# A gating unit's values moved ahead of the attention, and a gelu written with the hyperbolic tangent

## The chip, the cores and the metric

The kernel runs on one core of one Trainium2 chip. The metric is the device time of one execution in microseconds (us). The kernel before took 2144.43, 2147.16 and 2149.66 us in three runs; the median is 2147.16.

## The reference, cut to what matters

The program computes two stacks of two layers each on 256 tokens of width 1024. The change touches the mixer of the first stack (`first_block`), which runs once per layer. The mixer normalises its input, projects it with `w_in`, and splits the result for three units: a chunked spatial gating (a), a recurrence (b) and a sparse attention (c). Their outputs stand side by side and are projected back with `w_out`.

```python
def chunked_spatial_gating(z_a, ln_g, ln_b, w_s, b_s):
    u, v = split_cols(jax.nn.gelu(z_a), A_SIZES)
    u = u.reshape(Bn, nc, CHUNK, A_HEADS, HEAD_DIM)
    v = layer_norm(v.reshape(Bn, nc, CHUNK, A_HEADS, HEAD_DIM), ln_g, ln_b, LN_EPS)
    w = jnp.where(causal[None], w_s, 0.0)
    mixed = jnp.einsum('hts,bnshd->bnthd', w, v) + b_s.T[None, None, :, :, None]
    return (u * mixed).reshape(Bn, S, A_WIDTH)

for i in range(DEPTH):                        # DEPTH = 2
    z = rms_norm(h, g_mix[i]) @ w_in[i]
    z_a, z_b, z_c = split_cols(z, (A_COLS, B_COLS, C_COLS))
    y_a = chunked_spatial_gating(z_a, ...)    # 4 heads of 64
    y_b = rwkv7_time_mix(z_b, ...)            # 4 heads of 64, a state carried along the tokens
    y_c = nsa_attention(z_c, ...)             # 8 heads: compressed, selected and windowed keys
    h = h + jnp.concatenate([y_a, y_b, y_c], axis=-1) @ w_out[i]
    ...                                       # feed-forward (dense, then 8 experts) and one more gate
```

`jax.nn.gelu` is here the form 0.5 x (1 + tanh(sqrt(2/pi) (x + 0.044715 x^3))). The gating works per chunk of 128 tokens: it takes the values v, mixes them over the tokens of the chunk with a causal matrix, adds a bias, and multiplies by u.

## The kernel before, in words

All weights come from HBM as 32-bit numbers into raw tiles (`raw`), by loads that SyncE (SP) issues in a fixed order. Each raw tile is split into a high and a low part (`hl`): ScalarE (ACT) writes the high part, VectorE (DVE) the rest (`parts`, L392 and L393). A projection is then three matmuls for each product, so one of the 256-column projections `proj_fm` or `proj_tm` is 48 matmuls (`pj<-hl,xn` or `pj<-xn,hl`, `xn` being the normalised input).

`mix1` is the mixer. It projects the recurrence's input, runs the recurrence (`rwkv`, tiles in the bank `rw`), and projects for the other two units: `kv` (4), the queries `qT` (8 and 9), the values `vt` with the attention's gates, then, after the compression of keys and values (`nsa_cmp`), the gating's values `av` (5), the keys `ks` (7). Inside the attention (`nsa`), after the first of two halves of its heads, the function `between` projects the gating's other operand `uT` (6) and runs `gating`. The attention computes scores (`ns<-ks,qT`) with a mask (`ns<-cb,idb`), the maximum and exponential (L1139, L1142), transposes the weights and multiplies by the values (`py<-pT,vt`). `rows_out` and `route` multiply the result `y` with `w_out` (`pj<-y,hl`, `rw<-y,hl`); their first matmuls need only the recurrence's part of `y`.

`nsa_cmp` multiplies the keys and values by `cw1` in 32 steps (`ns<-cw,xp`), applies gelu (`hid`), transposes, multiplies by `cw2` (`kcT`, `vc`), scores against `qT` (`ns<-kcT,qT`), and takes an exponential (`pc`), whose transposes become `pcT`. The recurrence's output `yv` is normalised per head by `head_rs` (from the squares `gsq` to the reciprocal root `hrs`). `y` lies in a pool with one buffer (`act`) in which `xn` lies too, so it is written once the last reader of `xn` is done.

In `gating`, `gmws` (the mixing matrix) and `gmln` (the norm's gain and bias) are loaded, GpSimd masks `gmws`, ACT applies gelu to `uT` and `av`, DVE takes statistics per token and head (`gst`, `gmv`), ACT the root (`grs`), and DVE the four steps to `gvn` (L824 to L827). PE multiplies `ns<-gmws,gvn`, DVE adds the bias and multiplies by `uT` (`gm`), and `gm` becomes two of the eight parts of `y`.

The order of instructions on each engine is set when the program is built. A scheduler starts from the order of the code and lets an instruction that is ready pass one that is not, so that projections are strewn as fillers between the steps of the recurrence and of the attention. Each engine then works through its list in order; waits are for semaphores of other engines and of loads. ACT holds one table of functions at a time; a function of another table is preceded by ACT_TABLE_LOAD. Exponential and gelu need different tables here, and so does the root.

Of the kernel before, what the change touches and what calls it, by code (L numbers as in the profile page):

```python
# [28 lines left out]
AF = mybir.ActivationFunctionType  # L29
OP = mybir.AluOpType  # L30
AX = mybir.AxisListType

T = 256
# [249 lines left out]
class K:  # L283
# [511 lines left out]

    def gating(self, L, uT, v, y):

        nc, a = self.nc, self.a
        ws = self.t([128, 4, 128], "n2", "gmws")
        nc.sync.dma_start(ws, a["gmws"][L])  # L800
        lnb = self.t([128, 2, 256], "n2", "gmln")
        src = a["gmln"][L:L + 1]
        nc.sync.dma_start(lnb, bass.AP(tensor=src.tensor, offset=src.offset, ap=[[0, 128], [1, 512]]))
        bs = self.t([128, 2, 128], "n1", "gmbs")
        for h in range(4):
            src = a["gmbs"][L, h:h + 1]
            nc.sync.dma_start(bs[64 * (h % 2):64 * (h % 2) + 64, h // 2],
                              bass.AP(tensor=src.tensor, offset=src.offset, ap=[[0, 64], [1, 128]]))
        nc.gpsimd.tensor_tensor(ws, ws, self.cc("up_i").unsqueeze(1).to_broadcast([128, 4, 128]), op=OP.mult)
        nc.scalar.activation(uT, uT, AF.Gelu_apprx_tanh)  # L810
        nc.scalar.activation(v, v, AF.Gelu_apprx_tanh)
        st = self.t([128, 8, 6], "s", "gst")
        mv = self.t([128, 8, 2], "s", "gmv")
        v8 = v.rearrange("p j (h d) -> p (j h) d", h=4)
# [4 lines left out]
        rs = self.t([128, 8], "s", "grs")  # L819
        nc.scalar.activation(rs, mv[:, :, 1], AF.Sqrt, bias=self.cc("vec")[:, 4:5])  # L820
        nc.vector.reciprocal(rs, rs)
        vn = self.t([128, 2, 256], "n2", "gvn")
        vn8 = vn.rearrange("p j (h d) -> p (j h) d", h=4)
        nc.vector.tensor_tensor(vn8, v8, mv[:, :, 0:1].to_broadcast([128, 8, 64]), op=OP.subtract)  # L824
        nc.vector.tensor_tensor(vn8, vn8, rs.unsqueeze(2).to_broadcast([128, 8, 64]), op=OP.mult)
        nc.vector.tensor_tensor(vn, vn, lnb[:, 0:1].to_broadcast([128, 2, 256]), op=OP.mult)
        nc.vector.tensor_tensor(vn, vn, lnb[:, 1:2].to_broadcast([128, 2, 256]), op=OP.add)  # L827
        ps = self.bank("ns")
# [7 lines left out]
        mf = m.rearrange("p i j t -> p i (j t)")  # L836
        nc.vector.tensor_tensor(mf, mf, uT, op=OP.mult)
        self.dump(f"ya{L}", mf)
# [250 lines left out]
    def head_rs(self, s, scale, bias, floor=None):  # L1089


        nc, V = self.nc, self.nc.vector
# [4 lines left out]
        r = self.t([128, 8], "s", "hrs")  # L1097
        src = ps[:, :8]
        if floor is not None:
            V.tensor_scalar(r, src, floor, None, op0=OP.max)  # L1100
            src = r
        nc.scalar.activation(r, src, AF.Sqrt, scale=scale, bias=bias)
        V.reciprocal(r, r)
        p = self.bank("rw")
# [249 lines left out]
    def mix1(self, L, nxt):  # L1354
        a = self.a
        tp = self.tc.tile_pool
        with self.phase(f"m{L}", M1BANKS, "left", nm="ns", **M1ACC):
            with tp(name=f"wr{L}", bufs=1, reuse_waits="tile", side="right") as self.wr, \
                    tp(name=f"wp{L}", bufs=1, reuse_waits="tile") as self.wp:
                if L == 0:  # L1360
                    x = self.setup()
                else:
                    x = self.norm(self.pp(f"g_mix{L}", 0, 8))
# [19 lines left out]
                self.cycle = ("pj", "py")  # L1383
                self.proj_fm(a["w_in"][L, 4], x, kv)
                self.proj_fm(a["w_in"][L, 8], x, qT[:, 0:2])
                self.proj_fm(a["w_in"][L, 9], x, qT[:, 2:4])
                gps = self.t([128, 2, 24], "s4", "gps")
                self.proj_wide(a["w_vt"][L], x, vt, 24, gps)
                self.cycle = ("pj",)
                gt, vc, pcT = self.nsa_cmp(L, qT, kv, gps)  # L1390
                self.apply_rope(qT, qT, 0, "rp1")
                self.proj_tm(a["w_in"][L, 5], x, av)
                self.proj_fm(a["w_in"][L, 7], x, ks)
# [631 lines left out]
```

## Time and profile before

| | |
|---|---|
| median of three runs | 2147.16 us |
| the profiled execution's own time | 2147.74 us |
| its span | 2146.0 us |
| busy: PE, DVE, ACT | 96%, 77%, 60% of the span |
| mixer of layer 0 / layer 1 | about 0 to 206 / 420 to 640 us of the span |
| layer 1: first scores, then the product of the gating | 559.12, then 585.82 us |

The profile shows one execution, taken from the hardware. Rows of a timeline give start, duration, engine, line in the code, operation, the tiles (out<-in) and a count; in square brackets stands how long the engine waited before it and for whom. A matmul of 32-bit numbers that the code issues once can stand as two records. The granted clock of PE is 1.00 at its higher level (2.4 GHz) and 0.5 at its lower (1.2 GHz); a window with both lies between.

### The profile page before, as it was taken

How to read it: one execution, taken by the hardware profiler on the slowest of the kernel's cores; microseconds unless marked ns; L12 is line 12 of the kernel's file. 1: busy time of each engine (PE TensorE's matmuls, PEld its weight loads, DVE VectorE, ACT ScalarE, POOL GpSimd, SP SyncE). 2: the span in 40 equal slices, each digit the busy share in tenths (PEclk: the TensorE clock that was granted, in tenths of full speed). 3: DMA queues.
4: the chain of work that ended last, by engine and by line, in shares of the span. 5: the costliest groups of instructions: out<-in, count | busy, mean ns of one | idle time of the engine just before them, and what ended most of it. 6: DMA issues, size and time to landing. Idle time of an engine off the chain costs nothing.

```text
span 2146.0 us, 35556 instructions
## 1 busy us (share of the span) xinstructions
PE 2062.1 (96%) x14040; PEld 1828.6 (85%) x14040; DVE 1649.9 (77%) x2416; ACT 1292.8 (60%) x1914; POOL 28.6 (1%) x32
## 2 busy tenths in 40 slices
PE   7999999999898999999999999998999999999998
PEld 7877999988687888887887888787988999989998
DVE  7657888775747998989899888987858887756554
ACT  6347544552567777777877787776546444545443
POOL 0100000020000000000000000000000000000000
PEclk9999999999989999999999999998998999998999
DMA  6225999341426999899898989884347995435551
GB/s 244 83 70 187 322 341 331 136 151 52 177 84 221 367 347 340 337 367 338 335 355 340 369 322 358 345 325 148 122 179 265 349 337 185 130 138 167 187 182 55
DMA packets 106654, 519.84 MB, mean 242 GB/s; under 512 B 12400, under 2 KB 14448, under 8 KB 72432
## 3 DMA queue, kind: packets, MB, share of 16 engines
q1 hardware_dynamic: 106480, 517.50, 66.1%
q8 instruction: 112, 1.84, 0.3%
q14 instruction: 62, 0.51, 0.1%
HBM read 516.40 MB, written 1.05 MB: 241 GB/s over the span
## 4 chain that ended last, share of the span: by engine, by line
PE 62%; DVE 4%; ACT 2%; issue 1%; DVEq 0%; ACTq 0%
PE ps L346 37%; PE acc L346 17%; PE pj L346 3%; PE ac L346 2%; PE ns L346 2%; DVE hl L393 2%; PE ps L1624 1%; DVE ch L1697 1%; ACT hl L392 1%; PE py L346 0%; DVE xT L1603 0%; DVE xT L746 0%; ACT sq L565 0%; DVE xn L521 0%; PE ns L1155 0%
## 5 line engine op out<-in xcount | busy, mean ns | idle before, releaser
L393 DVE TENSOR_TENSOR hl<-raw,hl 128x1024 fp32r<-128x1024 f32 (+1 forms) x862 | 1028.9, 1224 | 222.6 <-ACT hl L392 217.9
L392 ACT CAST hl<-raw 128x1024 fp32r<-128x1024 f32 (+1 forms) x862 | 878.0, 1051 | 386.0 <-PE ps L346 193.3
L346 PE MATMUL ps<-hl,xe 128*128 128x512 f32 x2112 | 519.0, 400 | 6.3 <-ACTq L1639 4.2
L346 PEld LDWEIGHTS ps<-hl,xe 128*128 128x128 f32 x2112 | 390.6, 188 | 97.4 <-DVE hl L393 4.4
L346 PE MATMUL ps<-xn,hl 128*128 128x256 f32 x3552 | 433.2, 283 | 5.0 <-ACT xn L604 2.9
L346 PEld LDWEIGHTS ps<-xn,hl 128*128 128x128 f32 x3552 | 428.9, 191 | 6.3 <-ACT xn L604 3.5
L346 PE MATMUL acc<-hl,h 128*128 128x512 f32 x1056 | 262.2, 396 | 0.5 <-ACT h L1627 0.5
L346 PEld LDWEIGHTS acc<-hl,h 128*128 128x128 f32 x1056 | 198.7, 188 | 48.8 <-ACT h L1627 0.7
L346 PE MATMUL acc<-h,hl 128*128 128x256 f32 x1584 | 196.3, 283 | 0.0
L346 PEld LDWEIGHTS acc<-h,hl 128*128 128x128 f32 x1584 | 192.6, 192 | 0.2
L1668 DVE SCALAR_TENSOR_TENSOR junk<-raw,cact 128x1024 bf16<-128x1024 f32 x96 | 117.1, 1220 | 1.6 <-ACT cact L1662 0.7
L346 PE MATMUL pj<-xn,hl 128*128 128x256 f32 x720 | 102.9, 292 | 1.7 <-ACT xn L604 1.1
L346 PEld LDWEIGHTS pj<-xn,hl 128*128 128x128 f32 x720 | 92.6, 194 | 6.3 <-issue 3.9
L1620 ACT ACTIVATE s<-ps 128x256 f32<-128x256 f32 x88 | 33.9, 385 | 85.3 <-PE ps L346 85.2
L1627 ACT CAST h<-ps 128x256 fp32r<-128x256 f32 x88 | 32.7, 372 | 50.8 <-PE ps L1624 50.7
L1697 DVE SCALAR_TENSOR_TENSOR ch<-hp,par,ch 128x256 f32<-128x256 f32 x120 | 51.1, 477 | 0.0
L346 PE MATMUL ns<-xn,hl 128*128 128x256 f32 x288 | 40.0, 301 | 10.6 <-ACT hl L392 8.6
L346 PEld LDWEIGHTS ns<-xn,hl 128*128 128x128 f32 x288 | 38.5, 208 | 11.3 <-ACT hl L392 8.6
L346 PE MATMUL ac<-xn,hl 128*128 128x256 f32 x336 | 46.9, 290 | 0.3 <-ACT xn L604 0.3
L346 PE MATMUL pj<-y,hl 128*128 128x256 f32 x288 | 45.0, 293 | 0.9 <-ACT y L406 0.9
L346 PE MATMUL pj<-hl,xn 128*128 128x256 f32 (+2 forms) x288 | 44.4, 297 | 0.0
L346 PEld LDWEIGHTS ac<-xn,hl 128*128 128x128 f32 x336 | 43.7, 197 | 0.7 <-ACT xn L604 0.6
(478 smaller groups left out, 1990.2 us busy)
## 6 DMA issues: line engine op xcount, KB each, us to landing
raw<-moe SPq DMA_DIRECT2D x264, 1024.0 KB, 5.3
raw<-ffn SPq DMA_DIRECT2D x198, 512.0 KB, 5.0
raw<-ada SPq DMA_DIRECT2D x96, 512.0 KB, 5.8
raw<-w_in SPq DMA_DIRECT2D x76, 512.0 KB, 4.0
raw<-w_out SPq DMA_DIRECT2D x32, 512.0 KB, 3.3
raw<-ple_g SPq DMA_DIRECT2D x16, 512.0 KB, 4.6
cw<-cw SPq DMA_DIRECT2D x8, 512.0 KB, 5.0
c<-cst SPq DMA_DIRECT2D x2, 1536.0 KB, 6.5
```

The lines of the kernel that those rows point to most:

```text
L346: self.last = self.nc.tensor.matmul(out, l, r, start=start, stop=stop)
L392: nc.scalar.copy(t[:, 0, :n], r)
L393: nc.vector.tensor_tensor(t[:, 1, :n], r, t[:, 0, :n].bitcast(FT), op=OP.subtract)
L1620: nc.scalar.activation(s, ps[:, :T], AF.Silu)
L1624: nc.tensor.transpose(pt[:, b * 128:(b + 1) * 128], s[:, b * 128:(b + 1) * 128], self.cc("id"))
L1627: nc.scalar.copy(h[:, 0], pv)
L1668: self.nc.vector.scalar_tensor_tensor(self.junk, w, 1.0, self.cact, op0=OP.mult, op1=OP.mult, accum_out=self.mod[L][:, n:n + 1])
L1697: V.scalar_tensor_tensor(h[:, b], x, w, h[:, b], op0=OP.mult, op1=OP.add)
```

## The change

The projection of `av` moves up in `mix1`, right behind that of `kv`, and takes turns in the two banks `pj` and `py`. A new function `gate_values` follows the projection of `vt`: it loads `gmln`, applies gelu to `av`, and normalises it in place (no `gvn` any more). The root of the norm is ordered on ACT behind the root of `head_rs`. In `gating` the gelu of `uT` becomes three DVE steps, a hyperbolic tangent on ACT, and one more DVE step; the factor 0.5 goes into the last product. The tangent is in the table of the exponential.

```diff
@@ -793,21 +793,12 @@
                            nxt)
 
 
-    def gating(self, L, uT, v, y):
-
-        nc, a = self.nc, self.a
-        ws = self.t([128, 4, 128], "n2", "gmws")
-        nc.sync.dma_start(ws, a["gmws"][L])
+    def gate_values(self, L, v):
+
+        nc = self.nc
         lnb = self.t([128, 2, 256], "n2", "gmln")
-        src = a["gmln"][L:L + 1]
+        src = self.a["gmln"][L:L + 1]
         nc.sync.dma_start(lnb, bass.AP(tensor=src.tensor, offset=src.offset, ap=[[0, 128], [1, 512]]))
-        bs = self.t([128, 2, 128], "n1", "gmbs")
-        for h in range(4):
-            src = a["gmbs"][L, h:h + 1]
-            nc.sync.dma_start(bs[64 * (h % 2):64 * (h % 2) + 64, h // 2],
-                              bass.AP(tensor=src.tensor, offset=src.offset, ap=[[0, 64], [1, 128]]))
-        nc.gpsimd.tensor_tensor(ws, ws, self.cc("up_i").unsqueeze(1).to_broadcast([128, 4, 128]), op=OP.mult)
-        nc.scalar.activation(uT, uT, AF.Gelu_apprx_tanh)
         nc.scalar.activation(v, v, AF.Gelu_apprx_tanh)
         st = self.t([128, 8, 6], "s", "gst")
         mv = self.t([128, 8, 2], "s", "gmv")
@@ -817,14 +808,32 @@
         for n in range(8):
             nc.vector.bn_aggr(mv[:, n], st[:, n])
         rs = self.t([128, 8], "s", "grs")
-        nc.scalar.activation(rs, mv[:, :, 1], AF.Sqrt, bias=self.cc("vec")[:, 4:5])
+        root = nc.scalar.activation(rs, mv[:, :, 1], AF.Sqrt, bias=self.cc("vec")[:, 4:5])
+        self.tc.add_manual_dep(root.ins, self.root.ins.name, self.NOSYNC, reason="order on the engine")
         nc.vector.reciprocal(rs, rs)
-        vn = self.t([128, 2, 256], "n2", "gvn")
-        vn8 = vn.rearrange("p j (h d) -> p (j h) d", h=4)
-        nc.vector.tensor_tensor(vn8, v8, mv[:, :, 0:1].to_broadcast([128, 8, 64]), op=OP.subtract)
-        nc.vector.tensor_tensor(vn8, vn8, rs.unsqueeze(2).to_broadcast([128, 8, 64]), op=OP.mult)
-        nc.vector.tensor_tensor(vn, vn, lnb[:, 0:1].to_broadcast([128, 2, 256]), op=OP.mult)
-        nc.vector.tensor_tensor(vn, vn, lnb[:, 1:2].to_broadcast([128, 2, 256]), op=OP.add)
+        nc.vector.tensor_tensor(v8, v8, mv[:, :, 0:1].to_broadcast([128, 8, 64]), op=OP.subtract)
+        nc.vector.tensor_tensor(v8, v8, rs.unsqueeze(2).to_broadcast([128, 8, 64]), op=OP.mult)
+        nc.vector.tensor_tensor(v, v, lnb[:, 0:1].to_broadcast([128, 2, 256]), op=OP.mult)
+        nc.vector.tensor_tensor(v, v, lnb[:, 1:2].to_broadcast([128, 2, 256]), op=OP.add)
+
+    def gating(self, L, uT, vn, y):
+
+
+        nc, V, a = self.nc, self.nc.vector, self.a
+        ws = self.t([128, 4, 128], "n2", "gmws")
+        nc.sync.dma_start(ws, a["gmws"][L])
+        bs = self.t([128, 2, 128], "n1", "gmbs")
+        for h in range(4):
+            src = a["gmbs"][L, h:h + 1]
+            nc.sync.dma_start(bs[64 * (h % 2):64 * (h % 2) + 64, h // 2],
+                              bass.AP(tensor=src.tensor, offset=src.offset, ap=[[0, 64], [1, 128]]))
+        nc.gpsimd.tensor_tensor(ws, ws, self.cc("up_i").unsqueeze(1).to_broadcast([128, 4, 128]), op=OP.mult)
+        th = self.t([128, 2, T], "n2", "gth")
+        V.tensor_tensor(th, uT, uT, op=OP.mult)
+        V.tensor_scalar(th, th, 0.044715, 1.0, op0=OP.mult, op1=OP.add)
+        V.tensor_tensor(th, th, uT, op=OP.mult)
+        nc.scalar.activation(th, th, AF.Tanh, scale=math.sqrt(2 / math.pi))
+        V.scalar_tensor_tensor(uT, th, 1.0, uT, op0=OP.add, op1=OP.mult)
         ps = self.bank("ns")
         for h in range(4):
             for j in range(2):
@@ -834,7 +843,7 @@
         nc.vector.tensor_tensor(m, ps.rearrange("p (i j t) -> p i j t", i=2, j=2),
                                 bs.unsqueeze(2).to_broadcast([128, 2, 2, 128]), op=OP.add)
         mf = m.rearrange("p i j t -> p i (j t)")
-        nc.vector.tensor_tensor(mf, mf, uT, op=OP.mult)
+        V.scalar_tensor_tensor(mf, mf, 0.5, uT, op0=OP.mult, op1=OP.mult)
         self.dump(f"ya{L}", mf)
         self.split(y[:, 0, 0:2], y[:, 1, 0:2], mf)
 
@@ -1099,7 +1108,7 @@
         if floor is not None:
             V.tensor_scalar(r, src, floor, None, op0=OP.max)
             src = r
-        nc.scalar.activation(r, src, AF.Sqrt, scale=scale, bias=bias)
+        self.root = nc.scalar.activation(r, src, AF.Sqrt, scale=scale, bias=bias)
         V.reciprocal(r, r)
         p = self.bank("rw")
         for n in range(4):
@@ -1382,14 +1391,15 @@
                 qT = self.t([128, 4, T], "q4", "qT")
                 self.cycle = ("pj", "py")
                 self.proj_fm(a["w_in"][L, 4], x, kv)
+                self.proj_tm(a["w_in"][L, 5], x, av)
                 self.proj_fm(a["w_in"][L, 8], x, qT[:, 0:2])
                 self.proj_fm(a["w_in"][L, 9], x, qT[:, 2:4])
                 gps = self.t([128, 2, 24], "s4", "gps")
                 self.proj_wide(a["w_vt"][L], x, vt, 24, gps)
                 self.cycle = ("pj",)
+                self.gate_values(L, av)
                 gt, vc, pcT = self.nsa_cmp(L, qT, kv, gps)
                 self.apply_rope(qT, qT, 0, "rp1")
-                self.proj_tm(a["w_in"][L, 5], x, av)
                 self.proj_fm(a["w_in"][L, 7], x, ks)
 
                 def between():
```

The scheduler's order changes with it. PE, layer 0, in the recurrence of the kernel before: `X`, `MT`, `Vt`, `R`, `TT` are the recurrence's tiles, `hid` and `hT` the compression's, `pj<-hl,xn` the projection of `av`.

```order
L346 MATMUL pj<-hl,xn 128x256 x6
L346 MATMUL rw<-MT,X_842 64x64 x4
L346 MATMUL rw<-Vt,SC 128x128 x4
L1194 MATMUL ns<-cst,hid 128x64
L346 MATMUL pj<-hl,xn 128x256 x4
L346 MATMUL rw<-R,TT 128x128 x4
L346 MATMUL ns<-hT,cw_1208 128x32 x2
L346 MATMUL ns<-cw_1208,hT 32x64 x2
```

The transposes of `hid` and the products with `cw2` (`cw_1208`) stand between steps of the recurrence. In the kernel after they stand behind it, among the projection of `ks` (`pj<-xn,hl`) and behind the second product of `head_rs`:

```order
L346 MATMUL pj<-xn,hl 128x256 x4
L346 MATMUL rw<-cst,hrs 64x128 x8
L346 MATMUL pj<-xn,hl 128x256 x3
L1203 MATMUL ns<-cst,hid 128x64
L346 MATMUL pj<-xn,hl 128x256 x14
L346 MATMUL ns<-hT,cw_1297 128x32 x2
L346 MATMUL ns<-cw_1297,hT 32x64 x2
L346 MATMUL pj<-xn,hl 128x256
L346 MATMUL ns<-kcT,qT 128x32 x8
L346 MATMUL pj<-xn,hl 128x256 x36
```

The compression moved out of the recurrence; of its 32 steps with `cw1`, 25 stand behind the recurrence's end as well. All 48 matmuls of `av`, of which 27 stood beside the recurrence before, stand beside it now. In layer 1, 17 steps of the compression stand behind the recurrence's end, and all 48 matmuls of `av` (before 23) ahead of it.

PE, layer 1, up to the attention's first scores (`ns<-ks,qT`), before; `pj<-xn,hl x19` is `ks`, `x20` is `uT`:

```order
L346 MATMUL pj<-xn,hl 128x256 x19
L1257 MATMUL ns<-cst,pc 32x128 x6
L346 MATMUL ns<-ks,cst 128x512
L346 MATMUL py<-pcT,vc 128x512
L346 MATMUL pj<-xn,hl 128x256 x20
L346 MATMUL ns<-ks,qT 128x128 x4
```

And after:

```order
L1266 MATMUL ns<-cst,pc 32x128 x6
L346 MATMUL pj<-xn,hl 128x256 x3
L346 MATMUL ns<-ks,cst 128x512
L346 MATMUL py<-pcT,vc 128x512
L346 MATMUL pj<-y,hl 128x256
L346 MATMUL rw<-y,hl 128x256
L346 MATMUL pj<-y,hl 128x256 x5
L346 MATMUL rw<-y,hl 128x256 x17
L346 MATMUL pj<-y,hl 128x256 x6
L346 MATMUL rw<-y,hl 128x256 x2
L346 MATMUL ns<-ks,qT 128x128 x4
```

All of `uT` and 34 of 48 matmuls of `w_out` with the recurrence's part of `y` have come ahead of the first scores.

SP, layer 1, the loads around `gmws`, before (numbers are those of the tiles; `ple_p` and `moe` are weights of later stages):

```order
L365 DMA raw_6819<-ple_p 128x1024
L365 DMA raw_6824<-ple_p 128x1024
L365 DMA raw_6829<-moe 128x2048
L800 DMA gmws_6380<-gmws 128x512
L803 DMA gmln_6382<-gmln 128x512
L365 DMA raw_6831<-moe 128x2048
```

And after:

```order
L365 DMA raw_6832<-ple_p 128x1024
L365 DMA raw_6799<-w_out 128x1024
L365 DMA raw_6804<-w_out 128x1024
L365 DMA raw_6837<-moe 128x2048
L365 DMA raw_6839<-moe 128x2048
L365 DMA raw_6841<-moe 128x2048
L824 DMA gmws_6412<-gmws 128x512
L365 DMA raw_6843<-moe 128x2048
```

`gmws` moved behind two loads of `w_out` (which stood behind it before) and behind three of `moe`; `gmln` is loaded far ahead, beside the recurrence.

## Rows read from the trace of the kernel before

**Rows 1.** Page, part 1: busy us, share of span, instructions of each engine.

```profile
PE 2062.1 (96%) x14040; PEld 1828.6 (85%) x14040; DVE 1649.9 (77%) x2416; ACT 1292.8 (60%) x1914; POOL 28.6 (1%) x32
```

**Rows 2.** Windows: stretch, us, busy us (instructions) per engine, clock, DMA share, GB/s.

```profile
140.00:150.00 10.00, 10.00 (x54) 7.09 (x54) 4.73 (x13) 2.53 (x12) 0.00 (x0) 0.85 0.16 54
200.00:210.00 10.00, 10.00 (x87) 10.00 (x86) 9.34 (x17) 7.55 (x15) 0.00 (x0) 1.00 0.97 347
580.00:590.00 10.00, 4.18 (x27) 3.19 (x28) 7.49 (x11) 2.12 (x3) 0.00 (x0) 0.67 0.77 283
```

**Rows 3.** Timeline, PE, layer 0: start, us, engine, line, operation, tiles, count, [idle before].

```profile
126.83 1.09 PE L346 MATMUL rw<-cst,hrs 128*64 128x128 f32 x16 [1.43 <-DVE hrs L1103]
...
137.77 0.83 PE L1257 MATMUL ns<-cst,pc 128*32 128x128 f32 x6 [1.25 <-DVE pc L1251]
...
140.24 2.08 PE L346 MATMUL ns<-ks,cst 128*128 128x512 f32 x2
141.33 3.66 PE L346 MATMUL pj<-xn,hl 128*128 128x256 f32 x19
```

**Rows 4.** Timeline, PE, layer 0, gating's product and the scores after.

```profile
166.79 1.11 PE L346 MATMUL ns<-gmws,gvn 128*64 128x128 f32 x16 [1.11 <-DVE gvn L827]
...
169.57 1.13 PE L346 MATMUL ns<-ks,qT 64*128 64x256 f32 x4 [0.69 <-DVE gm L834]
```

**Rows 5.** Timeline, PE, layer 1, from the transposes of ks to the second half.

```profile
554.43 1.12 PE L346 MATMUL ns<-ks,cst 128*128 128x512 f32 x2 [0.37 <-DVE ks L616]
...
556.54 2.65 PE L346 MATMUL pj<-xn,hl 128*128 128x256 f32 x20
559.12 0.71 PE L346 MATMUL ns<-ks,qT 64*128 64x128 f32 x8
...
570.48 0.62 PE L346 MATMUL rw<-y,hl 128*128 128x256 f32 x3 [0.71 <-ACT y L406]
...
585.82 2.00 PE L346 MATMUL ns<-gmws,gvn 128*64 128x128 f32 x16 [6.06 <-DVE gvn L827]
587.75 1.23 PE L346 MATMUL ns<-ks,qT 64*128 64x128 f32 x8
...
589.45 2.07 PE L346 MATMUL ns<-ks,qT 64*128 64x256 f32 x4
```

**Rows 6.** Timeline, ACT, layer 1, first half of the attention.

```profile
569.81 0.62 ACT L406 CAST y<-yv 128x512 fp32r<-128x512 f32 x1 [1.88 <-PE pj L346]
...
571.85 1.28 ACT L810 ACT_TABLE_LOAD   x1
573.14 0.63 ACT L810 ACTIVATE uT<-uT 128x512 f32<-128x512 f32 x1
...
578.58 2.92 ACT L392 CAST hl<-raw 128x1024 fp32r<-128x1024 f32 x3
```

**Rows 7.** Timeline, DVE, layer 1, same stretch.

```profile
577.45 1.22 DVE L1146 TENSOR_TENSOR p<-p,sm 128x1024 f32<-128x1024 f32 x1
...
580.79 0.68 DVE L824 TENSOR_TENSOR gvn<-av,gmv 128x512 f32<-128x512 f32 x1
...
584.98 0.69 DVE L827 TENSOR_TENSOR gvn<-gvn,gmln 128x512 f32<-128x512 f32 x1
```

**Rows 8.** SP's issues, GpSimd's mask, and the landing of gmws (one tile's view).

```profile
567.35 0.44 SPq L800 DMA_DIRECT2D gmws<-gmws  x1
...
580.90 2.07 SPq L365 DMA_DIRECT2D raw<-w_out  x2
...
576.12 1.28 POOL L809 TENSOR_TENSOR gmws<-gmws,cst 128x512 f32<-128x512 f32 x1 [65.10 <-DMA gmws<-gmws]
...
DMA to landing us min/median/max: 5.8/7.2/8.6
```

**Rows 9.** Timeline, PE, layer 1, the compression's products.

```profile
518.50 1.07 PE L346 MATMUL ns<-cw,xp 128*32 128x128 f32 x16
...
537.68 1.87 PE L346 MATMUL ns<-kcT,qT 128*128 128x32 f32 x16
```

## The prediction

> **What bounds the kernel now.** I read the page first. TensorE (PE) is busy for 96% of the span [rows 1], and the change adds and removes no matmul: the products of the gating take `av` where they took `gvn`, and projections move. So the time can change only where PE stands idle, where it runs at the low clock, or where a chain of dependent steps holds it although the record says busy. The change touches one stage, the mixing of the first block, which runs twice: layer 0 over about 0 to 206 us, layer 1 over about 420 to 640.
>
> The windows of that stage come next. In layer 1, 580 to 590, PE is busy 4.18 of 10 us at a granted clock of 0.67, and in layer 0 the clock is 0.85 in 140 to 150 [rows 2]. The clock falls from its higher level to the lower one after a stretch in which PE waited, and doubles some durations: the two transposes of `ks` took 2.08 us there [rows 3] and 1.12 in layer 1 [rows 5].
>
> PE's timeline names the waits. Layer 0: 1.43 us for `hrs`, 1.25 for `pc` [rows 3], 1.11 for `gvn` [rows 4]. Layer 1: 0.37 for `ks`, 0.71 for `y`, then 6.06 for `gvn`, the largest [rows 5]. Why `gvn` is late is in the timelines of ScalarE (ACT) and VectorE (DVE): a table load and `uT`'s gelu stand between the exponentials, and three casts of weights fill 578.58 to 581.50 [rows 6], and the four steps of the normalisation stand between casts on DVE, so that the last ends at 585.67 [rows 7]. `gmws` had been issued at 567.35, landed 8.6 us later and was masked by 577.40 [rows 8]; it had slack.
>
> **The change part by part.** The sum stands against the profiled execution's own 2147.74 us (span 2146.0 and 1.74 around it); the median of the runs shown is 2147.16, 0.6 lower.
>
> *Gating values early.* Gelu, statistics, root and the four steps leave the attention. They now lie before it, in the recurrence or just behind it. In layer 1 the wait of 6.06 goes, and in layer 0 that of 1.11. With layer 1's wait goes the low clock behind it: the products took 2.00 against 1.11 in layer 0, the scores 1.23 against 0.71 in their first half, the next scores 2.07 against 1.13 in layer 0 [rows 4, 5]: 0.89 + 0.52 + 0.94 = 2.35 us. What is late next is `gmws`.
>
> *`gmws` later on its queue.* Before, one 1 MB load stood right ahead of it in the queue. Now two 512 KB loads for `w_out` and three 1 MB loads stand ahead of it in layer 1 (the last pair of fences in the section on the change). The `w_out` pair waits for a weight buffer, which by the order of DVE comes free 1 to 2.5 us after the attention's first scores. From there 4.25 MB come at the 283 GB/s of 580 to 590 [rows 2] in 15 us, at the 347 of 200 to 210, where the transfers filled 0.97 of their engines, in 12; masking on GpSimd takes 1.28 [rows 8]. So `gmws` is ready 14 to 19 us after the first scores. PE used to need 26.70 us from the first scores to the product (559.12 to 585.82), 19.93 without the waits of 6.06 and 0.71. Of its fillers there (28 for `uT`, 48 for `w_out`) 14 are left, and 62 at 2.65/20 = 0.133 us are 8.2 us, so 11.7 us of work remain [rows 5]. The softmax between scores and products cannot shrink that far: its maximum, exponentials and sums had those fillers as cover. I add 1.8 us, half of the 3.6 that lie between the start of the last exponentials (573.14 + 0.63 + another load of 1.28 = 575.05 [rows 6]) and the end of their weighting (577.45 + 1.22 = 578.67 [rows 7]); the bounds are nothing and the whole. PE arrives at 13.5. The new wait lies between 0 and about 6; I take 2, in the lower half, because the faster rate belongs to a stretch of nothing but such loads, as this one is.
>
> The Trainium skill (DMA: Bandwidth & Descriptors, "Two DMAs through the same engine are not ordered") says that descriptors of one queue on one engine start in order. That speaks against this part: whatever stands ahead of `gmws` is begun first. The two loads of `gmws` in the trace took 5.8 and 8.6 us [rows 8], the longer one behind the 1 MB load; that agrees, though it shows no wait of PE on them. Without the rule `gmws` would land in about those times and the wait would be 0.
>
> *`w_out`'s first products and `uT` before the attention of layer 1.* 34 matmuls for `w_out` and all 48 of `uT` now stand ahead of the first scores. PE's sum does not change by that. The wait of 0.71 for the cast of `y` goes: two groups of 1.12 us lie between its release and its reader, against a cast of 0.62 [rows 5, 6]. The attention starts later by 62 matmuls less the 25 of `av` that left, 37 x 0.133 = 4.9 us, which the fillers taken from it give back.
>
> *The projection of `av` inside the recurrence, the compression behind it.* In layer 0, 21 of `av`'s 48 matmuls come in (2.8 us), and 25 of 32 steps of the compression (two records each, 50 x 0.067 = 3.4 us by 1.07/16) with the scores behind them (1.87) go out [rows 9]. In layer 1, 25 of `av` come in (3.3 us) and 17 steps go out (34 x 0.067 = 2.3). Does the recurrence change by as much? If PE's own work sets its pace, what leaves it is paid behind it and the sum is zero. If the chain of dependent steps sets it, layer 0 loses 3.4 + 1.9 - 2.8 = 2.5 us and layer 1 gains 1.0. The share of busy time does not tell the two apart, since a PE with fillers is always busy. I take 0; the two ends together would be +1.5.
>
> *The waits behind the recurrence in layer 0.* The 1.43 us for `hrs` go: compression steps and `ks` now stand between its two products. The 1.25 for `pc` stay, as the compression is now later and its exponential still behind a table load; the bounds are that they vanish and that they grow by 3.6, the length of the softmax step above. The low clock there costs 2.08 - 1.12 = 0.96 and 3.66 - 19 x 0.133 = 1.13, together 2.1 [rows 3, 5]; as about half the waiting ahead of it goes, I take half, 1.05.
>
> *Tanh for gelu.* Four steps on DVE, each at most the 0.68 us of a `gvn` step [rows 7], and an activation that needs no other table than the exponential's. They lie ahead of the product's use, not of the product; the four steps of `gvn`, eight statistics and their sums leave the same place, so DVE has less to do there. Ten table loads fewer at 1.28 [rows 6] are 12.8 us of ACT, which was 60% busy [rows 1]; they count only by the waits above. The attention of layer 0 also loses 18 fillers (29 to 11 ahead of those for `w_out`), which covered between nothing and 18 x 0.133 = 2.4 us of its softmax; the low end is nearer, as 48 for `w_out` stay: +0.5.
>
> The Trainium skill (ScalarE: Activation LUTs, "What ACT_TABLE_LOAD costs") puts a switch at 2.66 us, a load of 1.28 and a drain. The trace shows 1.28 and the activation 0.01 us behind it, with no drain; by the Trainium skill's figure ten switches would be worth 26.6 us of ACT, still off PE's path.
>
> Sum: layer 1 -6.06 - 2.35 - 0.71 + 1.8 + 2.0 = -5.3; layer 0 -1.11 - 1.43 - 1.05 + 0.5 = -3.1. Together -8.4, and 2147.74 - 8.4 = 2139.3: **2139 us**.
>
> **Rivals.**
> *All of the waiting goes.* `gmws` comes in time and nothing new waits: layer 1 -9.1, layer 0 -1.11 - 2.68 - 2.1 = -5.9, so 2147.74 - 15.0 = 2132.7. For it: the load has 13 us, against 8.6 before. Against it: the softmax loses its cover.
> *The recurrence is bound by its chain.* Layer 0 then pays 2.5 for the compression behind it, and the wait for `pc` grows by 3.6: 2139.3 + 6.1 = 2145.4, no measurable change. For it: its products are small and each waits for a copy. Against it: it holds fillers at every step.
> *Slower: `gmws` behind the weights.* If the two `w_out` loads find their buffer only where they did before, at 580.90, 21.8 us after the first scores [rows 5, 8], then `gmws` is issued some 2 us later, lands 8.6 behind that and is masked at 33.7. PE would wait 33.7 - 13.5 = 20.2 instead of 2: 2139.3 + 18.2 = 2157.5. It decides from a wait of 2 + 8.4 = 10.4 us on, that is from `gmws` ready 24 us after the first scores. For it: in the trace that pair is the last to be issued before the product. Against it: in the new order the casts they wait for stand ahead of the softmax.
>
> **How the numbers follow.** The forecast 0.47, with an own range of 2133 to 2143; all waiting gone 0.17; bound by the chain 0.22; slower 0.14. A measurement of this kernel can tell 0.2%, 4.3 us: faster means below 2142.9, slower above 2151.5. Faster: 0.45 + 0.17 + 0.04 = 0.66. Same: 0.02 + 0.17 = 0.19. Slower: 0.01 and 0.14 = 0.15. The range from 2130 to 2151 leaves out the slower case and the far end of the best one.
>
> **What would show it.** In the profile after, the product `ns<-gmws,av` of layer 1 begins within 16 us of the first scores, and its wait, if any, is put down to GpSimd or the load. The clock of that stretch is 1.00. No `hrs` wait behind layer 0's recurrence. I am wrong if the stretch from the first scores to the product stays over 20 us in layer 1, or if the stretch before the first scores grows by over 7 us in either layer.

## The result, and the profile after

The kernel after takes 2138.95 us (median of 22 runs, 2129.49 to 2148.46), the kernel before 2149.43 in the same sets of runs (22, 2142.56 to 2159.05). The ratio is 0.9948 [0.9935, 0.9962], 10.5 us or 0.52% faster. The profiled execution took 2135.86 us, its span is 2134.1. The line of the engines on the page, against [rows 1] (PE is TensorE, PEld its weight loads):

```profile
PE 2058.0 (96%) x14040; PEld 1828.4 (86%) x14040; DVE 1655.0 (78%) x2424; ACT 1280.4 (60%) x1904; POOL 30.1 (1%) x32
```

The span of this execution is 11.9 us shorter with the same share busy: PE's busy time is 4.1 us shorter and its standing still 7.8 us. The window views of the kernel before and then after, one window for each layer from the first `rw<-yv,cst` behind the recurrence to the end of the mixer (columns as in [rows 2]):

```profile
120.82:205.80 84.98, 78.54 (x532) 60.57 (x531) 59.57 (x134) 56.31 (x121) 1.29 (x1) 0.98 0.38 127
...
535.80:627.41 91.61, 82.88 (x559) 64.94 (x558) 61.91 (x137) 57.87 (x127) 1.28 (x1) 0.94 0.37 135
```

```profile
116.92:198.30 81.38, 79.88 (x585) 63.26 (x584) 61.04 (x138) 49.51 (x120) 1.57 (x1) 1.00 0.36 125
...
526.46:610.75 84.29, 78.80 (x556) 62.12 (x555) 61.80 (x140) 48.40 (x122) 2.31 (x1) 0.98 0.35 133
```

Layer 0 got 3.60 us shorter here although more of PE's work lies in it (its busy time rose by 1.34), and its clock is now 1.00 throughout. Layer 1 got 7.32 shorter. PE's timeline of layer 0 after, the rows that answer to [rows 3, 4]:

```profile
122.71 1.09 PE L346 MATMUL rw<-cst,hrs 128*64 128x128 f32 x16
...
133.06 1.44 PE L346 MATMUL pj<-xn,hl 128*128 128x256 f32 x10 [0.78 <-DVE ks L616]
...
138.71 1.12 PE L346 MATMUL ns<-ks,cst 128*128 128x512 f32 x2
...
160.72 1.14 PE L346 MATMUL ns<-gmws,av 128*64 128x128 f32 x16
...
164.83 0.38 PE L346 MATMUL pj<-y,hl 128*128 128x256 f32 x1 [0.72 <-ACT y L406]
```

The waits for `hrs`, `pc` and `gvn` are gone, the two transposes of `ks` take 1.12 us instead of 2.08, and two waits are left, 1.50 us in all. Before there were eight between the recurrence and the mixer's end, 6.32 us: the 1.43, 1.25 and 1.11 of [rows 3, 4], and 0.56 (`av`), 0.34 (`pcT`), 0.71 (`y`), 0.69 (`gm`) and 0.23 (`y`). Layer 1 after, answering to [rows 5]:

```profile
540.54 3.68 PE L346 MATMUL pj<-xn,hl 128*128 128x256 f32 x29 [0.78 <-DVE ks L616]
...
555.43 0.71 PE L346 MATMUL ns<-ks,qT 64*128 64x128 f32 x8
...
566.80 1.13 PE L1164 MATMUL ns<-cst,p 128*128 128x128 f32 x8 [2.10 <-ACT p L1151]
568.80 2.88 PE L346 MATMUL py<-pT,vt 128*64 128x512 f32 x7 [0.86 <-ACT pT L1165]
571.41 0.34 PE L346 MATMUL ns<-gmws,av 128*64 128x128 f32 x1
...
572.69 0.71 PE L346 MATMUL ns<-ks,qT 64*128 64x128 f32 x8
...
574.84 1.13 PE L346 MATMUL ns<-ks,qT 64*128 64x256 f32 x4 [1.11 <-DVE gm L843]
```

From the first scores to the product of the gating it is 571.41 - 555.43 = 15.98 us, before 26.70. The waits are now for the exponentials and their copy (2.10, 0.86) and for `gm` (1.11); with 0.78 for `ks` that is 4.85 against 8.12 (6.06, 0.71 and 0.37 of [rows 5], and 0.98 for `pc`). The granted clock of the 15.98 us is 0.90, not 1.00 (columns as in [rows 2]):

```profile
555.43:571.41 15.98, 13.02 (x76) 9.08 (x77) 13.13 (x31) 9.74 (x37) 2.31 (x1) 0.90 0.85 341
```

The timeline of SP, GpSimd (POOL) and DVE around it, and the landing time of `gmws` (the tile's view: shortest, median, longest), answering to [rows 6 to 8]:

```profile
553.98 3.32 SPq L365 DMA_DIRECT2D raw<-w_out  x2
...
557.35 1.38 SPq L365 DMA_DIRECT2D raw<-moe  x3
558.77 0.72 SPq L824 DMA_DIRECT2D gmws<-gmws  x1
...
568.71 1.22 DVE L1155 TENSOR_TENSOR p<-p,sm 128x1024 f32<-128x1024 f32 x1
568.75 2.31 POOL L830 TENSOR_TENSOR gmws<-gmws,cst 128x512 f32<-128x512 f32 x1 [66.42 <-DVE sm L1284]
569.85 1.75 DVE L832 TENSOR_TENSOR gth<-uT 128x512 f32<-128x512 f32 x1
...
572.10 0.69 DVE L834 TENSOR_TENSOR gth<-gth,uT 128x512 f32<-128x512 f32 x1
```

```profile
DMA to landing us min/median/max: 4.0/6.9/9.8
```

The two loads of `w_out` are issued by 557.30, 1.87 us after the first scores. `gmws` is issued behind them and three 1 MB loads, lands 9.8 us later (568.6) and is masked by 571.06, 15.6 us after the first scores.

The change gives some of this back elsewhere. Behind layer 1's mixer, PE's work on the norm and the router (many of its products have 1 or 8 columns) took 30.10 us up to the first product of the experts, and takes 35.41 now. Its windows, before and then after:

```profile
620.00:630.00 10.00, 9.44 (x83) 9.27 (x81) 8.61 (x11) 8.32 (x16) 0.00 (x0) 1.00 0.94 359
630.00:640.00 10.00, 10.00 (x54) 10.00 (x54) 0.86 (x5) 1.60 (x4) 0.00 (x0) 0.56 0.16 62
640.00:650.00 10.00, 9.26 (x74) 9.01 (x73) 8.28 (x29) 8.05 (x14) 0.00 (x0) 0.93 0.01 3
```

```profile
610.00:620.00 10.00, 9.53 (x54) 9.36 (x53) 1.35 (x3) 3.41 (x9) 0.00 (x0) 0.62 0.43 178
620.00:630.00 10.00, 9.31 (x43) 9.02 (x44) 2.13 (x11) 2.85 (x5) 0.00 (x0) 0.50 0.00 1
630.00:640.00 10.00, 9.26 (x63) 8.98 (x64) 8.29 (x25) 7.72 (x16) 0.00 (x0) 0.85 0.01 2
```

By these clocks, before, about 10 us of that work ran at the lower level (1.2 GHz; 8.8 + 1.4), now about 20 (7.6 + 10 + 3); 10 us more at half the speed are 5 of the 5.31 us. PE is busy for over 9 of 10 us in each of these windows. No matmul in it was changed, but the scheduler put them in another order. The rows up to the first product with 256 columns, before and then after:

```profile
627.41 1.02 PE L346 MATMUL ns<-cst,sq 128*128 128x1 f32 x8 [0.56 <-DVE sq L572]
628.30 1.93 PE L346 MATMUL ns<-rw,xT 128*128 128x8 f32 x16
630.08 0.72 PE L346 MATMUL ns<-ph,hl 128*128 128x256 f32 x4
```

```profile
611.64 2.37 PE L346 MATMUL ns<-rw,xT 128*128 128x8 f32 x14
613.86 1.84 PE L346 MATMUL ns<-cst,sq 128*128 128x1 f32 x8
615.56 2.28 PE L346 MATMUL ns<-rw,xT 128*128 128x8 f32 x10
617.70 0.99 PE L346 MATMUL ns<-ph,hl 128*128 128x256 f32 x3
```

Before, 24 small products stand ahead of it; after, with the eight `ns<-cst,sq` at 610.75, 40.

### The profile page after: what moved, and what is told of

Read it like the earlier page. It is cut to its first block, busy times and chain, and to the rows that moved or that the text cites. A ratio compares the mean times of both kernels' runs of the same rounds, so it can differ in the third digit from the quotient of the medians.

```text
span 2134.1 us, 35568 instructions
## 1 busy us (share of the span) xinstructions
PE 2058.0 (96%) x14040; PEld 1828.4 (86%) x14040; DVE 1655.0 (78%) x2424; ACT 1280.4 (60%) x1904; POOL 30.1 (1%) x32
## 4 chain that ended last, share of the span: by engine, by line
PE 62%; DVE 4%; ACT 2%; issue 1%; DVEq 0%; ACTq 0%
PE ps L346 37%; PE acc L346 17%; PE pj L346 3%; PE ac L346 2%; DVE hl L393 2%; PE ns L346 2%; PE ps L1634 1%; DVE ch L1707 1%; ACT hl L392 1%; PE py L346 0%; DVE xT L1613 0%; DVE xT L746 0%; ACT sq L565 0%; DVE xn L521 0%; PE ns L1164 0%
## 5 line engine op out<-in xcount | busy, mean ns | idle before, releaser
L393 DVE TENSOR_TENSOR hl<-raw,hl 128x1024 fp32r<-128x1024 f32 x862 | 1028.7, 1224 | 223.1 <-ACT hl L392 218.6
L392 ACT CAST hl<-raw 128x1024 fp32r<-128x1024 f32 x862 | 878.5, 1051 | 408.5 <-PE ps L346 194.4
L346 PEld LDWEIGHTS ns<-xn,hl 128*128 128x128 f32 x288 | 38.4, 208 | 11.4 <-ACT hl L392 8.7
```

Source lines behind the costliest of these rows:

```text
L346: self.last = self.nc.tensor.matmul(out, l, r, start=start, stop=stop)
L392: nc.scalar.copy(t[:, 0, :n], r)
L393: nc.vector.tensor_tensor(t[:, 1, :n], r, t[:, 0, :n].bitcast(FT), op=OP.subtract)
```

## The experiments

In every kernel three stretches can be read from PE's timeline: both mixers (from the first `rw<-AR,be` of the recurrence to the mixer's end), the dense stage between them, and the norm and router behind the second. The starts of the experts' first products (`ps<-hl,xe`) include them all. Times are of one profiled execution each, ratios of medians against the kernel before.

| kernel | mixers | dense | router | experts start | ratio [95%] |
|---|---|---|---|---|---|
| before | 282.35 | 276.88 | 30.10 | 657.51 | |
| before again | 285.55 | 276.81 | 30.25 | 657.17 | 1.0001 [0.9977, 1.0025] |
| after | 267.92 | 275.42 | 35.41 | 646.16 | 0.9948 [0.9935, 0.9962] |
| after again | 272.79 | 275.41 | 33.99 | 649.65 | 0.9943 [0.992, 0.9966] |
| e1_values_late | 281.67 | 279.44 | 35.50 | 662.20 | 1.0011 [0.9989, 1.0032] |
| e2_proj_only | 276.57 | 280.05 | 33.00 | 654.01 | 0.9997 [0.998, 1.0014] |
| e3_tanh_only | 281.34 | 277.90 | 34.12 | 658.83 | 1.001 [0.9991, 1.0029] |
| e4_values_gelu | 269.38 | 280.05 | 35.53 | 652.25 | 0.9976 [0.996, 0.9993] |
| e5_gmws_early | 266.97 | 274.78 | 34.05 | 645.40 | 0.9968 [0.9951, 0.9985] |
| e6_u_early | 278.65 | 276.98 | 33.85 | 658.37 | 0.9983 [0.9967, 0.9998] |
| e7_held | 277.66 | 275.44 | 35.57 | 656.57 | 0.9996 [0.9985, 1.0008] |
| e8_both_early | 275.98 | 277.01 | 35.33 | 656.63 | 0.998 [0.9965, 0.9995] |
| e9_half_held | 273.32 | 275.38 | 32.20 | 648.51 | 0.9961 [0.9946, 0.9976] |
| e10_half_gm | 268.61 | 275.43 | 35.65 | 648.35 | 0.9939 [0.992, 0.9958] |

The two profiles of after differ by 4.9 us in the mixers alone, so one profile can't tell differences below that. To about that much the start of the experts follows the ratios: 11.4 us earlier in after against 11.2 by its ratio, 5.3 against 5.2 in e4; the widest gap is e5, 12.1 against 6.9. Some profiled executions lie far from the median of their kernel: e1's took 2155.98 us against 2147.11, e10's 2144.79 against 2136.0.

**Values late.** The projection of `av` and `gate_values` go back behind the compression; the tangent stays.

```diff
-                self.proj_tm(a["w_in"][L, 5], x, av)
...
-                self.gate_values(L, av)
                 gt, vc, pcT = self.nsa_cmp(L, qT, kv, gps)
                 self.apply_rope(qT, qT, 0, "rp1")
+                self.proj_tm(a["w_in"][L, 5], x, av)
+                self.gate_values(L, av)
```

> The gating's values are normalised early, but the projection of av stays where it was, behind the compression; the tanh form stays. Theory A (the gain is the vanished wait for gvn and the low clock behind it): layer 1's product no longer waits over 1 us for DVE, the stretch from the first scores to the product falls from 26.70 us to about 20 (28 fillers of uT are still in it), layer 0's recurrence stays at 52.6 us from its first AR,be to yv, and the time is 5 to 9 us below before. Rival B (the move of the projection, which takes the compression out of the recurrence, carries the gain): at most 3 us below before.

Measured: no change against before. PE's timeline of e1 in layer 1:

```profile
549.66 0.38 PE L1266 MATMUL ns<-cst,pc 128*32 128x128 f32 x2 [0.98 <-DVE pc L1260]
...
583.53 1.15 PE L346 MATMUL ns<-gmws,av 128*64 128x128 f32 x16 [0.34 <-POOL gmws L830]
```

The wait of 6.06 is gone (0.34 left) and scores to product fell from 26.70 to 20.70 us, but layer 0 kept its waits for `hrs`, `av`, `pc` and `y` (6.50 us in all there), and in this execution, 8.9 us above e1's median, the dense stage and the router gave back 8 us. The stretch came as theory A had it, the time as rival B had it (at most 3 us below): removing the largest wait of the profile, without the early projection, did not move the time. Layer 0's recurrence took 54.16 us where 52.6 was expected, at a clock of 0.97 (before 1.00).

**Projection only, and tangent only.** e2 is before with the projection of `av` moved up and the gating as it was; e3 is before with the tangent in `gating`.

```diff
                 self.proj_fm(a["w_in"][L, 4], x, kv)
+                self.proj_tm(a["w_in"][L, 5], x, av)
```

```diff
-        nc.scalar.activation(uT, uT, AF.Gelu_apprx_tanh)
+        th = self.t([128, 2, T], "n2", "gth")
...
+        nc.vector.scalar_tensor_tensor(uT, th, 1.0, uT, op0=OP.add, op1=OP.mult)
```

> Only the projection of av is moved ahead; its gelu, norm and the gelu of uT stay in the gating as before. Theory A (PE's own work paces the recurrence, so what leaves it shortens it and is paid behind it): layer 0's recurrence falls from 52.6 us to 49 to 50, the way from yv to the first scores grows by 1 to 3, and layer 1's product still waits 4 us or more for gvn; 0 to 4 us below before in all. Rival B (the recurrence is paced by its chain): it stays within 1 us of 52.6 and the time rises by 0 to 4 us. Rival C (the move carries the gain): 8 us or more below before.

> Only the gelu of uT is written with the tangent; the values stay in the gating. Theory A: the root of the norm still needs a table of its own between the exponentials, so layer 1's product still waits 4 us or more for gvn and the time stays within 3 us of before. Rival B (table loads are what made gvn late): the wait falls below 2 us and the time by 6 us or more.

Measured: neither changes the time. PE's rows for the product of the gating in layer 1, in e2 and then in e3:

```profile
580.34 1.12 PE L346 MATMUL ns<-gmws,gvn 128*64 128x128 f32 x16 [1.59 <-DVE gvn L827]
```

```profile
579.96 1.28 PE L346 MATMUL ns<-gmws,gvn 128*64 128x128 f32 x16 [2.50 <-DVE gvn L832]
```

Each alone shortens the wait of 6.06 and neither removes it; both expectations had it at 4 us or more and were wrong in that. Layer 0's recurrence takes 49.50 us in e2 and 52.64 in e3: 49.51 in after and 52.64 in before, so at a clock of 1.00 it follows the place of the projection.

**Values early, gelu kept.** After, with the activation in place of the tangent's steps.

```diff
-        nc.scalar.activation(th, th, AF.Tanh, scale=math.sqrt(2 / math.pi))
...
+        nc.scalar.activation(uT, uT, AF.Gelu_apprx_tanh)
```

> All of the change but the tangent: the values are early, the gelu of uT uses its own table. Theory A (the early values carry the gain; the tangent saves two loads that lie on a softmax without cover): layer 1 goes from the first scores to the product in 16 to 19 us, against 15.98 after and 26.70 before, and the time is 0 to 3 us above after. Rival B (the tangent is half of the gain): 5 us or more above after.

Measured: 0.24% faster than before, by the medians less than half of the change's gain, though the two intervals just meet (from 0.9960 here, up to 0.9962 in after). The mixers are within 1.5 us of after's. ACT, SP, GpSimd and PE in layer 1:

```profile
556.79 1.28 ACT L831 ACT_TABLE_LOAD   x1
...
563.12 1.28 ACT L1146 ACT_TABLE_LOAD   x1 [1.87 <-DVE mx L1143]
...
565.04 0.44 SPq L824 DMA_DIRECT2D gmws<-gmws  x1
...
574.21 2.03 PE L1159 MATMUL ns<-cst,p 128*128 128x128 f32 x8 [1.01 <-ACT p L1146]
...
576.80 1.27 POOL L830 TENSOR_TENSOR gmws<-gmws,cst 128x512 f32<-128x512 f32 x1 [68.92 <-DVE p L1150]
```

The two table loads are back, and the product comes 17.47 us after the first scores, as theory A had it; the time, 6 us above after by the ratios, is nearer to rival B's. In layer 0 the product waits 1.39 us for GpSimd's mask. The larger part of the difference to after in the table, 4.6 us, lies in the dense stage, which the tangent does not touch.

**`gmws` early.** Loaded and masked in `gate_values`, in a buffer of its own.

```diff
+        ws = self.ws = self.t([128, 4, 128], "gw", "gmws")
+        nc.sync.dma_start(ws, self.a["gmws"][L])
+        nc.gpsimd.tensor_tensor(ws, ws, self.cc("up_i").unsqueeze(1).to_broadcast([128, 4, 128]), op=OP.mult)
```

> The changed kernel with gmws loaded and masked beside the recurrence, in a buffer of its own. Theory A (in layer 1 gmws comes ready within 0.4 us of the moment PE needs it, so it costs next to nothing by itself, but GpSimd's mask and DVE's first tangent step slowed each other, 2.31 against 1.28 and 1.75 against 0.69 us): from the first scores to the product 15.4 to 16.0 us against 15.98, the first tangent step back to 0.7, PE's wait of 1.11 for gm below 0.5; 0 to 2 us below the changed kernel. Rival B (gmws is what the product waits for): the stretch falls below 14.5.

Measured: not faster than after. The product begins 12.90 us after the first scores, under rival B's 14.5, but only its first half moved (ahead of products with `vt`), so I compare the first scores with those of the second half: 17.26 us in after, 16.98 in after again, 16.66 in e5. DVE and PE in e5:

```profile
570.33 0.68 DVE L833 TENSOR_TENSOR gth<-uT 128x512 f32<-128x512 f32 x1
...
575.47 1.13 PE L346 MATMUL ns<-ks,qT 64*128 64x256 f32 x4 [0.60 <-ACT p L1152]
```

The first step of the tangent is back at 0.68 us, and the wait of 1.11 for `gm` became 0.60 for an exponential. By these rows the late `gmws` costs 0.3 to 0.6 us in layer 1; a profile of each can't show that in the time.

**`uT` early, and both.** e6 projects `uT` and takes its tangent ahead of the attention; e8 adds the early `gmws`.

```diff
+                self.proj_fm(a["w_in"][L, 6], x, uT)
+                self.gate_other(uT)
                 def between():
-                    self.proj_fm(a["w_in"][L, 6], x, uT)
                     self.gating(L, uT, av, y)
```

> The changed kernel with uT projected and its tangent taken ahead of the attention instead of in the gating. Theory A (the bias step of gm waits on DVE behind the tangent's last step, and PE waits 1.11 us for gm): that wait goes, the way from the product to the end of the mixer in layer 1 falls by about 1 us from 39.34, and the three steps that lie ahead of the scores lengthen nothing by more than 0.5. Rival B (the steps then stand before ks and the scores on DVE): yv to the first scores grows by 1 to 2 us in either layer and the sum is zero or worse.

> The changed kernel with gmws early and uT's tangent early together. Theory A: the two effects add, 1 to 3 us below the changed kernel over the two mixers, mostly between the product and the end of the mixer. Rival B (what leaves the gating is paid before the first scores): no gain in the sum from the start of the recurrence to the end of the mixer.

Measured: both lose most of the gain. From `yv` to the first scores of layer 0 e6 takes 29.90 us against after's 25.74, and in layer 1 its product comes 19.26 us after the scores, with more waits for exponentials (1.58 and 1.51 the longest) and a clock of 0.75 in that stretch. In layer 0, where after has no wait between the scores and the product, e6 has one of 3.30 us for an exponential: there `uT`'s matmuls are worth more as cover for the softmax than ahead of it. In layer 1 they stood ahead of the scores in after already, so the loss there is not shown to be theirs. The way from the product to the mixer's end, which theory A had 1 us shorter, is 41.43 us against 39.35.

**Products for `w_out` held back.** e7 orders all of its first 48 matmuls behind the first half's first masks, as cover for the softmax; e9 only the second 24; e10 is e9 with e5's `gmws`.

```diff
-            res = out(a["w_out"][L], y, (1, 0, 2, 3), after=last, nxt=nxt)
+            res = out(a["w_out"][L], y, (1, 0, 2, 3), after=self.scored, nxt=nxt)
```

> The changed kernel with the first 48 matmuls of w_out held behind the first mask of the attention, so that they fill the softmax and not the way to it. Theory A (the fillers that went ahead of the scores uncovered the softmax): in layer 1 PE's waits of 2.10 for the exponentials and 0.86 for the transposes' copy fall below 0.5 each, and the way from yv to the product stays at or below 44.95 us, as ks is ready 3 us after PE now runs dry. Rival B (those waits have another cause, the casts or the exponentials themselves): they stay, and the way to the product gets no shorter.

> The changed kernel with only the second 24 of w_out's 48 early matmuls held behind the first mask; 24 still lie between the transposes of ks and the scores, and the held ones fill the softmax. Theory A (a wait of 3 us ahead of the scores brought the low clock in the run that held all 48): PE does not wait over 0.5 us ahead of layer 1's scores, the clock stays at 1.00 there, the wait for the exponentials falls from 2.10 to about 1, and yv to the product takes 43.5 to 45 us against 44.95. Rival B (holding itself costs): 46 or more.

> The same with gmws loaded and masked beside the recurrence as well. Theory A: the gain on the two mixers adds to 1 to 3 us against the changed kernel. Rival B: what the earlier work saves is lost between the product and the end of the mixer, and the sum over the two mixers stays within 1 us of the changed kernel's 267.9.

Measured: e7 loses the whole gain; e9 and e10 stand with after, as rival B had it for e10 (mixers 268.61 against 267.92). PE's timeline of e7, then its windows:

```profile
555.14 1.23 PE L346 MATMUL ns<-ks,qT 64*128 64x128 f32 x8 [3.08 <-DVE ks L490]
```

```profile
550.00:560.00 10.00, 6.92 (x21) 3.54 (x22) 6.90 (x14) 3.27 (x11) 0.00 (x0) 0.76 0.73 281
560.00:570.00 10.00, 10.00 (x44) 7.40 (x44) 5.12 (x17) 3.54 (x16) 1.28 (x1) 0.56 0.77 321
```

The waits for the exponentials are gone, as theory A had it, but without these matmuls PE waits 3.08 us for `ks` ahead of the first scores. Behind that wait it runs at the lower clock for over 10 us: from `yv` to the product 50.25 us against 44.95, which theory A had as the most. In e9 the wait ahead of the scores is gone (43.87 us from `yv` to the product, in theory A's range), and a wait of 2.63 for `gm` with a low clock behind it takes its place.

**The same two again.**

> The changed kernel once more, beside the two others. Theory A (the low clock of layer 1's stage behind the mixer, 35.4 us against 30.1 in the first profile of before, is not the change's doing, since other kernels had 33 to 35.6 there): the stretches of the mixers come out within 1 us of the first profile, the one behind the mixer may be anything from 30 to 36. Rival B (the change causes it): 35 or more again, and the stretches in between the same.

> The kernel before once more, for a second profile. Theory A (waits and order are fixed by the program, the low clock is not): the recurrences, yv to the scores and the scores to the product come out within 0.7 us of the first profile (52.6, 24.1, 21.9 and 53.1, 23.3, 26.7), with the wait of about 6 us for gvn in layer 1 again, while the stretches behind the product, and behind the mixer of layer 1, may differ by 2 to 5 us with the clock.

Measured: the ratios repeat, the lengths within the kernel only partly. Layer 0's recurrence (49.52 and 52.64), the dense stage and, within 1.5 us, the router's gap (33.99 and 30.25) come again. Two expectations failed: the mixers of after again are 4.9 us from the first profile where 1 was allowed, and from `yv` to the first scores of layer 0 before again takes 25.62 us instead of 24.09. There the mixer of layer 0 is 3.0 us longer than in the first profile, and the granted clock behind its recurrence 0.94 instead of 0.98. Layer 1 behind its recurrence is 88.51 us in after again, 84.29 in the first. Its waits are nearly the same, 4.90 us; its granted clock is 0.92 instead of 0.98, with these windows in after again:

```profile
580.00:590.00 10.00, 10.00 (x49) 7.09 (x47) 5.03 (x15) 6.08 (x20) 0.00 (x0) 0.84 0.00 1
590.00:600.00 10.00, 10.00 (x51) 7.83 (x51) 4.45 (x9) 5.54 (x13) 0.00 (x0) 0.72 0.01 2
```

In layer 0 after again the product of the gating waits 0.58 us for the mask of `gmws`, which the first profile has not.

## Why the prediction was right, and where its parts were not

The time came out as forecast (2138.95 against 2139), and most of the signs that the prediction named are there: the product within 16 us of the first scores (15.98), no `hrs` wait, the stretch before the first scores of layer 1 longer by 5.65 where 4.9 was worked out (the printed order has 32 matmuls of `w_out` there, not 34, which makes it 4.7). One is not: the clock of the stretch from the scores to the product was to be 1.00 and is 0.90. The slower rival did not come, as the two `w_out` loads were issued 1.87 us after the first scores, inside the 1 to 2.5 of the forecast.

That the two times agree to 0.05 us is luck. The forecast took 8.4 us off one execution of 2147.74; the gain by the medians is 10.5 us, from 2149.43, and the 22 runs of after spread over 19 us. The parts do not agree so well, in us, from the two pairs of profiles:

| term | forecast | first pair | second pair |
|---|---|---|---|
| ahead of layer 0's recurrence | 0 | -0.8 | +2.9 |
| mixer of layer 0 | -3.1 | -6.7 | -9.1 |
| mixer of layer 1 | -5.3 | -7.7 | -3.6 |
| dense stage | 0 | -1.5 | -1.4 |
| norm and router behind layer 1 | 0 | +5.3 | +3.7 |
| start of the experts | -8.4 | -11.4 | -7.5 |

The first row is the start of that recurrence in the span (68.18 and 64.56 us before, 67.41 and 67.46 after).

*Layer 0 was mis-sized.* The prediction took two of the three named waits away and let the 1.25 for `pc` stay, and it took half of the low clock's 2.1 us. All three went, and with them four of five smaller ones that it had not counted: 6.32 us became 1.50 (one for `y` stayed, one for `ks` came), and the clock rose from 0.98 to 1.00. The two rows from which the 2.1 was worked out overlap by 0.99 us, so it is too much: 0.02 of 84.98 us is 1.7, and nothing of that is left. That is -4.8 - 1.7 = -6.5, against -6.7 in the first pair; the -9.1 of the second holds the 3.0 us by which layer 0 was longer in before again. e1 and e3, with the projection where it was, keep the waits for `hrs`, `av` and `pc`; e2 and e4, with it early, have no `hrs` or `av` wait.

*The recurrence is paced by PE's own work.* It lost 3.13 us in layer 0 (52.64 to 49.51), where 2.5 was worked out. What left it is paid behind it: there PE's busy time rose by 1.34 us, and by 3.0 if the 1.7 of low clock before are taken out. In layer 1 it lost 0.38 where 1.0 more was worked out, but before stood at a clock of 0.98 there: against e3, with the projection late and the clock at 1.00 (52.29), after's 52.73 is 0.4 longer. So the sum of zero held, and the rival of a binding chain fell; in both profiles PE waits less than a microsecond in all through layer 0's recurrence.

*Layer 1 was right in size, between its two pairs.* The waits for `gvn` and `y` went as forecast, and so did the low clock at the three rows named, 2.35 us. New low clock came ahead of the product, 0.10 of 15.98 us, or 1.6. The softmax without its fillers cost 2.10 + 0.86 = 2.96 instead of 1.8, within its bounds. `gmws` was ready at 15.6 us, inside the 14 to 19, yet its price was 0.3 to 0.6 instead of 2.0 (e5), because PE itself came to the product only at 15.98 instead of 13.5, late by the softmax and the low clock. The rest of layer 1's gain depends on where the clock falls, which differs between executions of one kernel (0.98 of 84.29 us and 0.92 of 88.51, against 0.94 of 91.61 before).

*The router was not in the sum.* The prediction put nothing there and gave no reason. It gave back 3.7 to 5.3 us, and by luck offset most of what layer 0 gained beyond its term. Why the low clock lasts longer there in after was not settled: all the altered kernels show 32 to 36 us, before twice 30. It is shown that the products are the same and that their clock is lower, not what lowers it. A rival that no run separates is the order: both profiles of before have 24 small products ahead of the first with 256 columns, all the altered kernels, the tangent alone (e3) among them, 40 or 48. It can't be the whole, as e9 has after's order and takes 32.20 us against 35.41.

*No part alone moved the time.* The values with the tangent (e1), the projection (e2) and the tangent (e3) are each within 0.11% of before; projection and values together (e4) give 0.24%, all three 0.52%.

*The tangent's gain is only partly explained.* Without it e4 has 0.24% of the 0.52%, with intervals that just meet. In the mixers it is worth 1.5 us by one profile, less than two profiles can tell. The rest lies in the dense stage, 280.05 us against 275.4, at a clock of 0.98 against 0.99, and no run separates why. Alone (e3) it gives nothing.

## What to carry over

A wait removed from a PE that is 96% busy can be worth its own length and the low clock behind it, as in layer 0, but the largest one alone may bring nothing (e1); so count all the small waits of a stage. Moving fillers ahead of a chain takes its cover away; moving them behind it lets PE wait ahead of it (e7), so half of each may do as well as all of one. Sum the stages behind the change too: where their many small products run at either level of the clock, they can return a third of the gain (5.3 of 14.4 us) though no line of theirs was edited; and compare the order on PE there as well, which the scheduler had changed.

## What the hardware showed that was not expected

GpSimd's mask took 2.31 us where it took 1.28 before [rows 8], and a DVE step of the tangent 1.75 instead of 0.68. The mask was issued 0.04 us behind DVE's weighting of `p` (568.71 to 569.93) and is 1.03 us longer than before; the tangent's first step came at 569.85, and is 1.07 longer, ending 0.54 behind the mask. The Trainium skill (SBUF — State Buffer, "Who interferes with whom") says that a DVE instruction with two inputs in SBUF and a GpSimd instruction that reads SBUF block each other, the first to issue going first. The trace agrees: both lose about what the one ahead of them still had to run (1.18 us for the mask, 1.21 for the step), after again repeats it (2.35 and 1.75), and e5, which takes the mask out of that place, shows 0.68 again.

The two windows of 10 us around and behind a wait of 3.08 us (e7) have a granted clock of 0.76 and 0.56. Behind layer 1's mixer the clock was 0.50 to 0.62 in windows where PE was busy for 9.3 to 10 of 10 us, with products of 1 and 8 columns among its work. And the dense stage, which no edit touched, went from 274.78 us (e5, clock 0.99) to 280.05 (e2 and e4, 0.98): PE ran the same products in the same order in all three, with a busy time of 267.25 us and then 272.5 and an idle time of 7.5 and 7.6.
